# The output projection of the first 1024 tokens: moved wholly to the end of the recurrence

## The chip, the cores and the metric

The kernel runs on one core of a Trainium2 chip. The metric is the device time of one execution in microseconds (us), given as the median of several runs. The projections and the products of the MLP are done on pairs of float16 numbers: an operand is split into a high and a low part, and three products (high x high, low x high, high x low) stand for one product in float32.

## The reference

One layer of a hybrid encoder over 2048 tokens of width 1024:

```python
h = rmsnorm(x, norm_mix_g[l])
proj = h @ w_in[l]
u, dq, dk, dv, cq, cf, ci, cg = split_projection(proj)
y_a = s5_mixer(u, ...)          # 256 columns
y_b = diff_attention(...)       # 6 heads, 384 columns
y_c = hgrn2_mixer(cq, cf, ci, cg, ...)   # 6 heads, 384 columns, a recurrence over chunks of tokens
mix = jnp.concatenate([y_a, y_b, y_c], axis=-1)
x = x + (mix @ w_out[l])
h = rmsnorm(x, norm_ffn_g[l])
x = x + conv_glu_ffn(h, w_up[l], w_gate[l], conv_w[l], conv_b[l], w_down[l])
return rmsnorm(x, final_norm_g)
```

The change concerns `x + mix @ w_out` for tokens 0 to 1023, and the sums of squares that the second `rmsnorm` needs of them.

## The kernel before

**Two streams.** The program is written as two streams that a helper, `weave` (L2067), interleaves step by step by given weights. The left stream, `fore`, holds the input projections and attention, first for the queries of tokens 0 to 1023, then for those of 1024 to 2047. The right stream holds the S5 layer, the recurrence (`phase_hgrn`) and the tail (`phase_tail`: output projection, gated MLP, final norm). A step of the recurrence has weight 2.5, one of the tail 1.0, one unit of attention's second half 0.62, times `K.pace`, which is 1.8 in the head of the tail and 1.0 otherwise. A scheduler in the framework then fixes the order of instructions on every engine, the program order being the priority. DMAs are issued nearly all from SP's queue, in its order; among them are attention's transposing copies (L900).

**The recurrence** works in 12 units: three pairs of heads (`pr`), each with four chunks of 512 tokens (`j`), unit u = 4 pr + j. A unit has `proj`, `pre` and `fin`; `fin` stores its part of the mix at `Yd[5 + pr]` (L1360). After the loop `rest()` does `fin(10)`, `pre(11)` and `fin(11)`. Its pools: `g_w` (one weight buffer), `g_st` (one buffer for a raw weight), `g_h` (two buffers for the input), `g_3` and `g_2` (small tiles, tags `vn`, `x` and so on), and one PSUM buffer `g_pj` for projections.

**The mix** lies in DRAM as `Yd`: eight blocks of 128 columns, high and low part, by token. Blocks 0 and 1 are S5's, 2 to 4 attention's (one for each pair of heads), 5 to 7 the recurrence's. The weights `w_out` are used as q = 0 to 3 (two blocks each) and n = 0, 1 (512 output columns each); a pair (n, q) is one load of 512 KB and one split into high and low (`K.split`: a pass on ScalarE, L54, and one on VectorE, L62).

**`early_mix`** is woven with `rest()` and uses the recurrence's pools. It takes tokens 0 to 511 and q = 0, 1, 3 (`EARLY`). It loads two tiles of `Yd` (`o_ye`, 12 loads) into the `g_h` buffers, six weight pairs, and then goes over n and four token tiles: 18 matmuls into the one PSUM buffer (`o_pe`, L1409), an eviction that adds x (`o_re`, L1414), and a store into a side area of `Xd` (rows from 2048 on, L1417). `until(2)` before it waits, in program order, until two of attention's head pairs have been stored.

**The tail's head, `first`,** starts with the missing q = 2 for tokens 0 to 511 (`project(0, ...)`), onto the partial sums loaded back from `Xd` (`residual`, L1457). Then `project(1, ...)` does all four q for tokens 512 to 1023. `project` holds four PSUM banks at a time, loads `Yd` and `w_out` anew for every (n, q), and ends with `onto`: an eviction into `o_r` (L1500) and a sum of squares on ScalarE (`squares`, L1588). `keep` (L1941) stores the finished rows in `Xd`. `scaled` does the normalisation, `turned` transposes by TensorE (L1531), and the sinks `left` and `right` make of the first and second 512 tokens the seven operand quarters `f_q` of a Strassen-like product (`f_join`, L1554). `left` runs between the halves of `project(1)`. Then `activations` starts: 22 x 7 products of 12 matmuls each (`f_pm`, L98) and the elementwise work between them.

After `activations` comes the down product (`f_pd`, L1772) for these tokens, then the same for tokens 1024 to 2047, whose projection (`second`) also uses `project`.

**Room.** The tail's pools lie on the side of SBUF that the recurrence's pools held, with waits tile by tile; `f_q` comes first, where `g_w`, `g_st` and `g_h` were.

Of the kernel before, what the change touches and what calls it, by code (L numbers as in the profile page):

```python
# [18 lines left out]
S = 2048  # L19
# [14 lines left out]
EARLY = [0, 1, 3]  # L34
# [978 lines left out]
def phase_hgrn(K, Hd, w_in, lb_logits, norm_g, Yd, spare):  # L1013
# [9 lines left out]
    with ExitStack() as es:  # L1023
# [349 lines left out]
        yield from weave(rest(), 18, spare(pj, st, wp, hp, w3, w2), 6)  # L1373


def early_mix(K, x, w_out, Yd, Xd, pj, st, wp, hp, w3, w2):

    nc = K.nc
    y = []
    for a in range(2):  # L1380
        t = hp.tile([128, 2, KD, 256], F16, tag="h", name="o_ye")
        for k in [k for q in EARLY for k in (2 * q, 2 * q + 1)]:
            nc.sync.dma_start(out=t[:, :, k], in_=Yd[k, :, :, 256 * a:256 * a + 256])
        y.append(t)
    w4 = wp.tile([128, 4, 2, 2, 512], F16, tag="w", name="o_we")
    ws = [w4[:, i] for i in range(4)]
    ws += [w2.tile([128, 2, 2, 512], F16, tag="x", name="o_wx") for _ in range(2 * len(EARLY) - 4)]
    for i, w in enumerate(ws):
        n, q = divmod(i, len(EARLY))
        q = EARLY[q]  # L1390
# [6 lines left out]
    for n in range(2):  # L1397
        cc = slice(512 * n, 512 * n + 512)
        for t in range(4):
            rows = slice(128 * t, 128 * t + 128)  # L1400
            tk = slice(128 * (t % 2), 128 * (t % 2) + 128)
            r = w3.tile([128, 512], F32, tag="vn", name="o_re")
            nc.sync.dma_start(out=r, in_=x[0, rows, cc])
            ps = pj.tile([128, 512], F32, tag="j", name="o_pe")
            i = 0
            for q, w in zip(EARLY, ws[len(EARLY) * n:]):
                for k in range(2):
                    for a, b in ((0, 0), (0, 1), (1, 0)):
                        nc.tensor.matmul(  # L1409
                            out=ps, lhsT=y[t // 2][:, a, 2 * q + k, tk], rhs=w[:, b, k, :],  # L1410
                            start=(i == 0), stop=(i == 6 * len(EARLY) - 1),
                        )
                        i += 1
            nc.vector.scalar_tensor_tensor(  # L1414
                out=r, in0=ps, scalar=IWS / YS, in1=r, op0=ALU.mult, op1=ALU.add
            )
            nc.sync.dma_start(out=Xd[S + 128 * t:S + 128 * t + 128, cc], in_=r)  # L1417
            yield 1


def phase_tail(K, x, Xd, Yd, Ad, w_out, norm_g, W, conv_w, conv_b, w_down, final_g, out, es,
               ahead):

    tc, nc = K.tc, K.nc
# [690 lines left out]
```

## Time and profile before

| what | us |
|---|---|
| three timed runs | 2808.53, 2815.44, 2818.59 |
| their median | 2815.44 |
| the profiled execution | 2795.69 |
| its span, first to last instruction | 2794.0 |
| TensorE matmuls busy in it | 2442.0 (87%) |
| VectorE busy | 2004.2 (72%) |
| ScalarE busy | 1222.2 (44%) |
| GpSimd busy | 1309.4 (47%) |
| mean granted TensorE clock | 0.931 of full speed |

The profile is of one execution, so its stages are measured on its own 2795.69 us. PE is TensorE's matmul stream and PEld its weight loads, DVE is VectorE, ACT ScalarE, POOL GpSimd, SPq the queue from which SyncE issues DMAs. In a row for a group of instructions the operands stand as output<-input by tile name, then the shapes and a count. In a timeline the first number is the start, the second the length, and brackets hold the idle time before and what ended it. In a table by stage every engine has its busy time and, in parentheses, its instructions; behind them stand the granted clock, the mean busy share of the 16 DMA engines, and the GB/s that they moved. Matmuls are pipelined, so the length of one is longer than its distance from the next.

### The profile page before, as it was taken

The page shows a single profiled execution, that of the slowest core. Times are in us where ns is not written, and L with a number is a line of the kernel's source. Part 1 is how long each engine was busy: PE and PEld are TensorE (multiplying, and loading weights), DVE is VectorE, ACT ScalarE, POOL GpSimd, SP SyncE. Part 2 cuts the span into 40 slices and gives each one's busy share as a digit, 9 for nine tenths or more (in the row PEclk, how much of TensorE's full clock was granted, in tenths as well). Part 3 has the DMA queues.
Part 4 walks back from the last instruction along what each step waited for, and adds up shares of the span by engine and source line. Part 5 has one row for each costly group of instructions (what it writes and reads, how often), then busy time and mean ns, then how long its engine had stood idle before and what let it go on. Part 6 is the DMA issues. An engine that isn't in the chain of part 4 may idle for free. (4 is left out here: it accounts for less than half of the span.)

```text
span 2794.0 us, 42749 instructions
## 1 busy us (share of the span) xinstructions
PE 2442.0 (87%) x15438; PEld 1375.0 (49%) x15438; DVE 2004.2 (72%) x3893; ACT 1222.2 (44%) x2231; POOL 1309.4 (47%) x1095
## 2 busy tenths in 40 slices
PE   5998897989988888677998887859899999999998
PEld 3654546867766764243443333324344444444443
DVE  7466746789988897688779899975654855555575
ACT  5333344556645663565345555552234422222221
POOL 4788602334334432246666666631802344444180
PEclk8999998989989988788999999979999999999999
DMA  6675554555464656864455655587775655554733
GB/s 226 232 219 192 162 174 101 123 131 132 90 150 98 132 130 134 253 171 120 164 172 158 175 140 159 142 256 239 258 268 192 221 164 154 166 155 143 270 103 121
DMA packets 554533, 474.13 MB, mean 170 GB/s; under 512 B 276880, under 2 KB 432848, under 8 KB 553296
## 3 DMA queue, kind: packets, MB, share of 16 engines
q1 hardware_dynamic: 532144, 431.02, 54.1%
q10 hardware_dynamic: 22176, 40.38, 4.0%
q8 instruction: 121, 1.98, 0.3%
q14 instruction: 92, 0.75, 0.1%
HBM read 289.30 MB, written 127.93 MB: 149 GB/s over the span
## 5 line engine op out<-in xcount | busy, mean ns | idle before, releaser
L98 PE MATMUL f_pm<-f_q,f_w 128*128 128x512 f16 x3696 | 841.3, 387 | 37.9 <-DVE f_u L1837 21.7
L98 PEld LDWEIGHTS <-f_w 128*128 128x128 f16 x3696 | 363.7, 99 | 506.7 <-issue 90.4
L1772 PE MATMUL f_pd<-f_dw,f_da 128*128 128x512 f16 x1848 | 406.5, 383 | 11.7 <-DVE f_r L1750 10.4
L893 POOL TENSOR_TENSOR t_sc<-t_sc 128x1024 f16<-128x1024 f32 (+7 forms) x144 | 250.2, 1749 | 338.9 <-ACT t_sc L892 313.5
L1772 PEld LDWEIGHTS <-f_da 128*128 128x128 f16 x1848 | 181.8, 99 | 233.0 <-issue 18.5
L850 ACT ACTIVATE t_sc<-t_sc,t_nm 128x128 f32<-128x128 f32 (+7 forms) x192 | 229.1, 1195 | 99.1 <-DVE t_nm L845 91.7
L834 PE MATMUL t_ps<-t_k,t_q 96*128 96x512 f16 (+2 forms) x480 | 168.7, 377 | 99.0 <-DVE t_mx L838 86.6
L838 DVE CUSTOM_DVE_ANT_0 t_sc<-t_ps,t_base,t_mx 128x512 f32<-128x512 f32 (+3 forms) x288 | 185.1, 643 | 28.2 <-PE t_ps L834 21.5
L60 DVE TENSOR_TENSOR f_a<-f_t,f_a 128x512 f16<-128x512 f32 x132 | 148.1, 1129 | 46.1 <-ACT f_a L54 42.0
L98 PE MATMUL g_pq<-g_h,g_w 128*128 128x256 f16 x1152 | 158.6, 298 | 16.7 <-DVE g_sg L1162 10.6
L915 PE MATMUL t_po<-t_v,t_wt 128*128 128x64 f16 x2448 | 123.2, 201 | 56.4 <-DMA t_wt<-t_sc 48.7
L915 PEld LDWEIGHTS <-t_wt 128*128 128x128 f16 x2448 | 109.2, 104 | 123.1 <-DMA t_wt<-t_sc 67.0
L1837 POOL TENSOR_TENSOR f_t<-f_t,f_t 128x512 f32<-128x512 f32 x66 | 106.8, 1632 | 129.3 <-ACT f_a L54 108.3
L1487 PE MATMUL o_pm<-o_w,o_y 128*128 128x512 f16 x624 | 147.1, 394 | 19.9 <-DMA o_y<-Yd 14.1
L869 DVE SCALAR_TENSOR_TENSOR t_sc<-t_sc,t_a 128x1024 f32<-128x1024 f32 (+7 forms) x144 | 163.2, 1159 | 0.9
L1837 POOL TENSOR_TENSOR f_k<-f_k,f_k 128x512 f32<-128x512 f32 x88 | 124.7, 1417 | 73.2 <-ACT f_k L1869 68.3
L98 PE MATMUL g_pv<-g_w,g_h 128*128 128x256 f16 x1152 | 151.5, 288 | 8.0 <-ACT g_w L54 4.7
L62 DVE SCALAR_TENSOR_TENSOR f_dw<-f_db,f_dw 128x1536 f16<-128x1536 f32 (+1 forms) x36 | 104.1, 2910 | 73.8 <-ACT f_dw L54 73.7
L1837 POOL TENSOR_TENSOR f_db<-f_db 128x1536 f32<-128x1536 f32 (+1 forms) x32 | 128.2, 4044 | 60.6 <-DMA f_db<-in_w_down_dram 60.6
L892 ACT CAST t_sc<-t_sc 128x1024 f16<-128x1024 f32 (+7 forms) x144 | 112.1, 793 | 93.1 <-DVE t_sc L869 89.5
L54 ACT ACTIVATE f_w<-f_sum 128x512 f16<-128x512 f32 x110 | 69.2, 629 | 182.4 <-DVE f_sum L141 76.9
L54 ACT ACTIVATE f_a<-f_t 128x512 f16<-128x512 f32 x154 | 95.5, 628 | 114.5 <-POOL f_t L1837 56.6
(327 smaller groups left out, 4534.8 us busy)
## 6 DMA issues: line engine op xcount, KB each, us to landing
f_w<-Wd SPq DMA_DIRECT2D x231, 256.0 KB, 3.0
Wd<-f_w SPq DMA_DIRECT2D x154, 256.0 KB, 2.1
Ad<-f_a ACTq DMA_DIRECT2D x154, 256.0 KB, 2.8
f_da<-Ad SPq DMA_DIRECT2D x42, 768.0 KB, 4.4
g_h<-Hd SPq DMA_DIRECT2D x24, 1024.0 KB, 7.0
f_db<-in_w_down_dram SPq DMA_DIRECT2D x24, 768.0 KB, 10.5
o_wst<-in_w_out_dram SPq DMA_DIRECT2D x32, 512.0 KB, 5.4
o_y<-Yd SPq DMA_DIRECT2D x52, 256.0 KB, 4.7
```

The source lines that it names most:

```text
L54: nc.scalar.activation(out=hi, in_=src, func=AF.Copy, scale=scale)
L60: nc.vector.tensor_tensor(out=lo, in0=src, in1=hi, op=ALU.subtract)
L98: nc.tensor.matmul(out=out, lhsT=lhs(a, k), rhs=rhs(b, k), start=(n == 0), stop=(n == 3 * nk - 1))
L834: nc.tensor.matmul(out=ps[:, 0:k1 - k0], lhsT=qt[:, c, 128 * (i % 4):128 * (i % 4) + 128], rhs=H.k[:, c, k0:k1], start=True, stop=True,)
L838: V.tensor_tensor_reduce(out=sc[c][:, k0:k1], in0=ps[:, 0:k1 - k0], in1=bs[:, k0:k1], scale=1.0, scalar=-3e38 if j == 0 else mx[:, c, j - ...
L850: nc.scalar.activation(out=sc[c][:, 0:L], in_=sc[c][:, 0:L], func=AF.Exp, scale=SLOPES[h], bias=nm[:, c:c + 1], accum_out=H.la[:, c, n_:n_ ...
L869: V.scalar_tensor_tensor(out=sc[0][:, k0:k1], in0=sc[1][:, k0:k1], scalar=a[:, 1:2], in1=sc[0][:, k0:k1], op0=ALU.mult, op1=ALU.add,)
L893: nc.gpsimd.tensor_tensor(out=hl[:, LM + k0:LM + k1], in0=sc[0][:, k0:k1], in1=hl[:, k0:k1], op=ALU.subtract,)
L915: nc.tensor.matmul(out=po, lhsT=wt[:, w, b, :], rhs=vt[:, b, 64 * v:64 * v + 64], start=(b == 0 and w + v == 0), stop=(b == i and w == 1),)
L1487: nc.tensor.matmul(out=ps[t], lhsT=y[:, k, a, 128 * t:128 * t + 128], rhs=w[:, b, k, :], start=(q == qs[0] and i == 0), stop=(q == qs[-1] ...
L1772: nc.tensor.matmul(out=ps[t], lhsT=a[:, q, x, tk], rhs=w[:, y, q, :], start=(first and q + x + y == 0), stop=(last and q == n - 1 and y == 1),
L1837: eng.tensor_tensor(out=o, in0=a, in1=b, op=op)
```

## The change

`early_mix` now does the whole projection of tokens 0 to 1023: all four q, both chunks `c` of 512 tokens. The eight weight pairs are loaded and split once and stay on chip: four in the `g_w` buffer, two in a new pool `o_z`, two in the tag `x` of `g_2`. Each tile is 24 matmuls into the same single PSUM buffer, then the eviction that adds x, a sum of squares on ScalarE into a lasting tile `ss`, and a store of final rows in `Xd`. The `Yd` tiles of the second chunk take the two `g_h` buffers that the first chunk's had. It has 16 steps instead of 8, woven at 16 against the 18 of `rest()`, where it was 6. The tail's head has no projection left: it loads the eight row tiles back, takes the sums from `ss`, scales, turns and makes the quarters, `left` wholly before `right`. `until(3)` moves ahead of the early mix.

```diff
-        yield from weave(rest(), 18, spare(pj, st, wp, hp, w3, w2), 6)
+        more = pool("o_z", 1)
+        yield from weave(rest(), 18, spare(more, pj, st, wp, hp, w3, w2), 16)
...
     w4 = wp.tile([128, 4, 2, 2, 512], F16, tag="w", name="o_we")
     ws = [w4[:, i] for i in range(4)]
-    ws += [w2.tile([128, 2, 2, 512], F16, tag="x", name="o_wx") for _ in range(2 * len(EARLY) - 4)]
+    ws += [more.tile([128, 2, 2, 512], F16, tag=f"z{i}", name="o_wz") for i in range(2)]
+    ws += [w2.tile([128, 2, 2, 512], F16, tag="x", name="o_wx") for _ in range(2)]
     for i, w in enumerate(ws):
-        n, q = divmod(i, len(EARLY))
-        q = EARLY[q]
+        n, q = divmod(i, 4)
...
+    for c in range(2):
+        y = []
+        for a in range(2):
+            t = hp.tile([128, 2, KD, 256], F16, tag="h", name="o_ye")
+            t0 = CH * c + 256 * a
+            for k in range(KD):
+                nc.sync.dma_start(out=t[:, :, k], in_=Yd[k, :, :, t0:t0 + 256])
+            y.append(t)
+        for n in range(2):
+            cc = slice(512 * n, 512 * n + 512)
+            for t in range(4):
+                rows = slice(CH * c + 128 * t, CH * c + 128 * t + 128)
+                tk = slice(128 * (t % 2), 128 * (t % 2) + 128)
+                r = w3.tile([128, 512], F32, tag="vn", name="o_re")
+                nc.sync.dma_start(out=r, in_=x[0, rows, cc])
+                ps = pj.tile([128, 512], F32, tag="j", name="o_pe")
+                i = 0
+                for q in range(4):
+                    for k in range(2):
+                        for a, b in ((0, 0), (0, 1), (1, 0)):
+                            nc.tensor.matmul(
+                                out=ps, lhsT=y[t // 2][:, a, 2 * q + k, tk],
+                                rhs=ws[4 * n + q][:, b, k, :], start=(i == 0), stop=(i == 23),
+                            )
+                            i += 1
+                nc.vector.scalar_tensor_tensor(
+                    out=r, in0=ps, scalar=IWS / YS, in1=r, op0=ALU.mult, op1=ALU.add
+                )
+                sq = more.tile([128, 512], F16, tag="sq", name="o_sq")
+                nc.scalar.activation(
+                    out=sq, in_=r, func=AF.Square, scale=D ** -0.5, accum_out=ss[:, c, n, t:t + 1]
+                )
+                nc.sync.dma_start(out=Xd[rows, cc], in_=r)
+                yield 1
...
-                st, wp, yp = pool("f_st", 2), pool("f_w", 3), pool("o_y", 2)
-                tp, rp, fp = pool("f_t", 2), pool("f_r", 4), pool("f_f", 2)
+                rp, fp = pool("f_r", 8), pool("f_f", 2)
                 K.pace = 1.8
                 left, right = sinks(hc, fp, 4, 3)
-                r0, r1 = [], []
-                s0, s1 = sums(), sums()
-                yield from project(
-                    0, [q for q in range(4) if q not in EARLY], st, wp, yp, (pm,), onto(r0, s0, tp),
-                    lambda: r0.extend(residual(rp, Xd[S:S + CH])))
+                r0, r1 = [residual(rp, Xd[CH * c:CH * c + CH]) for c in range(2)]
                 xs = spread(hc, 1) + spread(hc, 3)
-                keep(r0, 0)
-                scaled(r0, xs, s0)
-                yield from project(1, range(4), st, wp, yp, (pm,), onto(r1, s1, tp),
-                                   lambda: r1.extend(residual(rp, x[0, CH:N])),
-                                   turned(xs, (pm,), left))
-                keep(r1, CH)
-                scaled(r1, r1, s1)
+                scaled(r0, xs, ss[:, 0])
+                scaled(r1, r1, ss[:, 1])
+                yield from turned(xs, (pm,), left)
                 yield sum(turned(r1, (pm,), right))
...
+    ss = const.tile([128, 2, 2, 4], F32, name="ss")
...
             def spare(*pools):
-                until(2)
-                yield from early_mix(K, x, w_out, Yd, Xd, *pools)
+                until(3)
+                yield from early_mix(K, x, w_out, Yd, Xd, ss, *pools)
...
-            until(3)
             yield None
```

More of the change, by code (lines that the diff above doesn't have):

```diff
@@ L33 @@
 SLOPES = [2.0 ** (-8.0 * (i + 1) / NH) for i in range(NH)]
-EARLY = [0, 1, 3]
 DOWN_PARTS = [3, 3, 3, 2]
@@ L1371, in rest, with early_mix @@
             yield from fin(11)
-        yield from weave(rest(), 18, spare(pj, st, wp, hp, w3, w2), 6)
-def early_mix(K, x, w_out, Yd, Xd, pj, st, wp, hp, w3, w2):
+        more = pool("o_z", 1)
+        yield from weave(rest(), 18, spare(more, pj, st, wp, hp, w3, w2), 16)
+def early_mix(K, x, w_out, Yd, Xd, ss, more, pj, st, wp, hp, w3, w2):
     nc = K.nc
[L1379 to L1384, printed above, removed]
     w4 = wp.tile([128, 4, 2, 2, 512], F16, tag="w", name="o_we")
     ws = [w4[:, i] for i in range(4)]
-    ws += [w2.tile([128, 2, 2, 512], F16, tag="x", name="o_wx") for _ in range(2 * len(EARLY) - 4)]
+    ws += [more.tile([128, 2, 2, 512], F16, tag=f"z{i}", name="o_wz") for i in range(2)]
+    ws += [w2.tile([128, 2, 2, 512], F16, tag="x", name="o_wx") for _ in range(2)]
     for i, w in enumerate(ws):
-        n, q = divmod(i, len(EARLY))
-        q = EARLY[q]
+        n, q = divmod(i, 4)
         f = st.tile([128, 2, 512], F32, tag="wst", name="o_wst")
@@ L1396, in early_mix @@
         K.split(w[:, 0], w[:, 1], f, WS)
[L1397 to L1418, printed above, removed]
@@ L1421, in phase_tail @@
-def phase_tail(K, x, Xd, Yd, Ad, w_out, norm_g, W, conv_w, conv_b, w_down, final_g, out, es,
+    for c in range(2):
[32 more added lines that the diff above has]
+                yield 1
@@ L1422, in phase_tail @@
+def phase_tail(K, x, Xd, ss, Yd, Ad, w_out, norm_g, W, conv_w, conv_b, w_down, final_g, out, es,
                ahead):
@@ L2014 @@
     Ud = tc.dram_tile([S, 256], F32, name="Ud")
-    Xd = tc.dram_tile([5 * CH, D], F32, name="Xd")
+    Xd = tc.dram_tile([S, D], F32, name="Xd")
+    ss = const.tile([128, 2, 2, 4], F32, name="ss")
     Ad = [[tc.dram_tile([128, MF // 2, 2, CH], F16, name=f"Ad{j}{i}") for i in range(7)]
@@ L2046, in spare @@
             def spare(*pools):
-                until(2)
-                yield from early_mix(K, x, w_out, Yd, Xd, *pools)
+                until(3)
+                yield from early_mix(K, x, w_out, Yd, Xd, ss, *pools)
             for _ in phase_hgrn(K, Hd, w_in, hgrn_lb_logits, hgrn_norm_g, Yd, spare):
                 yield LW[3]
-            until(3)
             yield None
-            for n in phase_tail(K, x, Xd, Yd, Ad, w_out, norm_ffn_g, W, conv_w, conv_b, w_down,
+            for n in phase_tail(K, x, Xd, ss, Yd, Ad, w_out, norm_ffn_g, W, conv_w, conv_b, w_down,
                                 final_norm_g, out, es, lambda: run(fore)):
```

## The prediction

> **What bounds the kernel now.** I read the page from the top (span, then the slices), then the busy times by stage, then single instructions of the stages that the change touches.
>
> ```profile
> span 2794.0 us, 42749 instructions
> ...
> PE   5998897989988888677998887859899999999998
> ```
>
> A slice is 70 us. TensorE leads almost everywhere; from slice 27 (about 1890 us) on it has nothing left to give. The dip in slices 15 to 18 is the place of this change: the recurrence's last units, then the tail's projection of tokens 0 to 1023, then the start of the tail's up products. I cut it into stages:
>
> ```profile
> core 0: us, PE busy (x) PEld busy (x) DVE busy (x) ACT busy (x) POOL busy (x), PEclk, DMA share, GB/s
> 1022.00:1057.00 35.00, 27.57 (x237) 16.49 (x237) 34.95 (x74) 21.67 (x36) 17.10 (x12) 0.76 0.67 163
> 1057.00:1102.00 45.00, 40.38 (x313) 22.85 (x313) 35.81 (x92) 16.48 (x27) 10.94 (x10) 0.96 0.56 141
> 1102.00:1140.00 38.00, 16.29 (x123) 7.59 (x124) 23.46 (x66) 13.52 (x23) 10.19 (x6) 0.60 0.61 115
> 1140.00:1190.00 50.00, 40.55 (x259) 18.79 (x259) 28.09 (x55) 27.41 (x47) 11.38 (x6) 0.86 1.03 306
> 1190.00:1236.00 46.00, 37.25 (x247) 19.88 (x246) 36.74 (x101) 28.47 (x58) 14.40 (x11) 0.93 0.62 174
> 1236.00:1287.00 51.00, 31.07 (x189) 17.65 (x189) 48.67 (x75) 31.45 (x58) 32.38 (x21) 0.70 0.46 112
> 1287.00:1450.00 163.00, 152.58 (x758) 69.04 (x758) 120.89 (x152) 68.60 (x117) 103.37 (x71) 0.99 0.49 160
> 1450.00:1815.00 365.00, 304.50 (x1753) 141.10 (x1752) 329.84 (x509) 197.72 (x330) 241.34 (x153) 0.94 0.56 158
> 1815.00:1861.00 46.00, 16.49 (x151) 8.65 (x150) 39.49 (x69) 25.11 (x35) 19.97 (x12) 0.62 0.80 238
> ```
>
> The reader is to see three limits. In 1022 to 1057 VectorE is full. In 1102 to 1140 nobody is: the last recurrence unit is a chain of dependent steps, TensorE idles 21.7 of 38 us. In 1140 to 1190 the DMA engines are full (share 1.03), with TensorE idle 9.5 us. From 1236 VectorE is full again (48.67 of 51), making the quarters `f_q`. From 1287 the up products run beside the second half of attention, and 1815 to 1861 is what is left of attention, with TensorE idle 29.5 us.
>
> **What is removed.** Both kernels issue 384 matmuls for these tokens: 144 + 48 + 192 before, 16 tiles of 24 after. Their price is that of one in a dense run:
>
> ```profile
> 1166.50 7.04 PE L1487 MATMUL o_pm<-o_w,o_y 128*128 128x512 f16 x24 [2.13 <-DMA o_y<-Yd]
> ...
> 1206.33 7.93 PE L1487 MATMUL o_pm<-o_w,o_y 128*128 128x512 f16 x36
> ...
> 1287.61 6.80 PE L98 MATMUL f_pm<-f_q,f_w 128*128 128x512 f16 x24
> ```
>
> 7.93/36 = 0.22 us (the listed 0.38 us of one is its latency). 240 matmuls, 240 x 0.22 = 53 us, leave the stages 1140 to 1236 and go to the end of the recurrence. Weight splits fall from 16 to 8, each 1.05 us of ScalarE (the next row) and 1.2 us of VectorE (a row further down), so 8.4 and 9.7 us go.
>
> ```profile
> L54 ACT ACTIVATE o_we<-o_wst x4: 1048/1054/1057, 1020.7 to 1049.3; 128x1024 f16<-128x1024 f32 x4
> ```
>
> The partial sums in `Xd` (written at L1417, read at L1457) stay one store and one load; the 8 stores of `keep` (L1941) go, since early_mix writes the final rows. Weight loads fall by 8 x 512 KB and `Yd` loads from 12 x 128 + 20 x 256 KB to 32 x 128 KB, which empties the DMA stage 1140 to 1190. The sums of squares, 16 on ScalarE, only move, from stages where it is busy 27.4 of 50 and 28.5 of 46 us to ones where it is busy 16.5 of 45 and 13.5 of 38; each hides under the next tile's matmuls, and the last one is on the path before and after alike. Their result now stays in the constant tile `ss`, so the normalisation of either chunk can start without waiting for a pass over loaded rows. `until(3)` costs nothing: the third attention pair, its last store below, was done 200 us earlier.
>
> ```profile
> 798.65 0.52 SPq L950 DMA_DIRECT2D Yd<-t_yo  x1
> ```
>
> **When the new early mix ends.** Its tiles today:
>
> ```profile
> 1052.90 1.21 DVE L62 SCALAR_TENSOR_TENSOR o_we<-o_wst,o_we 128x1024 f16<-128x1024 f32 x1
> 1056.67 0.68 DVE L1414 SCALAR_TENSOR_TENSOR o_re<-o_pe,o_re 128x512 f32<-128x512 f32 x1
> ...
> 1076.85 0.69 DVE L1414 SCALAR_TENSOR_TENSOR o_re<-o_pe,o_re 128x512 f32<-128x512 f32 x1 [0.43 <-PE o_pe L1409]
> 1087.93 0.68 DVE L1414 SCALAR_TENSOR_TENSOR o_re<-o_pe,o_re 128x512 f32<-128x512 f32 x1
> ...
> 1101.57 0.69 DVE L1414 SCALAR_TENSOR_TENSOR o_re<-o_pe,o_re 128x512 f32<-128x512 f32 x1 [0.95 <-PE o_pe L1409]
> ```
>
> Four weight tiles now gate the first output tile; the fourth is split at 1054.1, so tile 1 leaves PSUM at about 1057. From 1056.67 to 1101.57 six tiles of 18 matmuls took 7.5 us each; six more matmuls make 8.8 us. The recurrence ends at 1130, with its last store:
>
> ```profile
> 1129.95 0.53 SPq L1360 DMA_DIRECT2D Yd<-g_yo  x1
> ```
>
> Until then that gives 1 + 73/8.8 = 9.3 tiles. The other 6.7 run with attention alone: 24 x 0.22 = 5.3 us, 0.7 eviction, about 1 us of hand-over both ways (one PSUM buffer, `pj`), a tenth for attention: 7.6 us, 51 us in all. **End: 1181 us**, bounds 1153 (7.5 and 5.3 us a tile) and 1223 (the worst interval above, 11.1 us, for all 15). The second token chunk needs both `g_h` buffers back; its first eight loads go out while the last two tiles of the first chunk run, so they lie under TensorE work; uncovered, the eight would cost some 8 x 0.6 us of issue and a landing. On SP they stand in one queue with attention's transposes:
>
> ```profile
> L1383 SPq DMA_DIRECT2D o_ye<-Yd x12: 527/610/1162, 993.8 to 1024.1; - x12
> ```
>
> The early mix issued 12 + 6 + 8 + 8 = 34 DMAs there and issues 32 + 8 + 16 + 16 = 72; 38 more at up to 0.61 us are 23 us of SP's time over some 160 us. They hold up nothing as long as each is ready when its turn comes. A load that waits at SP's head for a buffer (`o_ye` for the first chunk's matmuls, `o_re` for a store) stops the transposes behind it, and with them attention's value matmuls; I price that with attention, below.
>
> **From there to dense up products.** Today the last projection matmuls end here
>
> ```profile
> 1225.82 0.59 PE L1487 MATMUL o_pm<-o_w,o_y 128*128 128x512 f16 x2
> ```
>
> at 1226.2 (the start of the last), and the products run densely from 1287.6: 61.4 us of norms, turns and quarters, VectorE-bound. None of it is removed. The chain gains a trip through DRAM:
>
> ```profile
> Xd<-o_re SPq DMA_DIRECT2D x8, 256.0 KB, 2.5
> o_r<-Xd SPq DMA_DIRECT2D x4, 512.0 KB, 6.9
> ```
>
> 2.5 + 6.9 = 9.4 us. `left`, which ran under the projection's second half, now runs behind it, but under that trip: 8 steps of 0.69 + 0.63 us on ScalarE are 10.6 us. I count 9.4 once (bounds 0, and 20 if the trip, `left` and later weight loads, whose room is now under `f_r`, add up). Dense products: 1181 + 61.4 + 9.4 = 1251.8, that is **36 us earlier**.
>
> ```profile
> L1562 ACT ACTIVATE f_q<-o_pt,o_g x16: 667/686/732, 1197.7 to 2134.6; 128x512 f32<-128x512 f32 x16
> ```
> and for the split behind each of them
> ```profile
> L54 ACT ACTIVATE f_q<-f_join x40: 612/630/675, 1201.6 to 2189.5; 128x512 f16<-128x512 f32 x40
> ```
>
> **What is given back.** Attention filled these stages. These rows count its score matmuls by stage (the second pair of columns is their weight loads):
>
> ```profile
> 1236.00:1287.00 51.00, 7.34 (x18) 1.94 (x19) 0.70 0.46 112
> 1287.00:1450.00 163.00, 4.07 (x11) 0.98 (x10) 0.99 0.49 160
> 1450.00:1815.00 365.00, 34.62 (x100) 9.60 (x99) 0.94 0.56 158
> 1815.00:1861.00 46.00, 8.52 (x16) 1.66 (x16) 0.62 0.80 238
> ```
>
> and these the up products `f_pm` in two of the stages:
>
> ```profile
> 1287.00:1450.00 163.00, 149.45 (x672) 22.50 (x33) 13.78 (x24) 0.99 0.49 160
> 1450.00:1815.00 365.00, 274.49 (x1120) 35.06 (x52) 23.50 (x41) 0.94 0.56 158
> ```
>
> In 36 us attention made 36 x 18/51 = 12.7 scores; they now fall beside the up products. With p for a product and s for a score, 163 = 672p + 11s and 365 = 1120p + 100s give s = 1.14 us. By the weave's sums 3.4 of the 12.7 stay until after the last up product: the new early mix adds 8 steps of 2.5, worth 20/0.62 = 32 units of attention, while the tail's head shrinks from 66 steps (10 projections of 5, and 16 for the two turns) to 16, at 1.8 x 0.62 worth 59 and 14; 13 units fewer, 3.8 units a score (212 units and 56 scores a head). In the rest stage a score takes 46/16 = 2.9 us. So 9.3 x 1.14 + 3.4 x 2.9 = 20.5 us come back (bounds 0, if they fit into idle time, and 12.7 x 2.9 = 37).
>
> **Sum:** 36 - 20.5 = 15.5 us. After 1861 nothing changes. The profiled execution took 2795.69 us (1.7 around its span), so 2780 on its scale; the median of the three timed runs is 2815.44, 19.75 higher, and I carry that over: **2800 us**.
>
> **Rivals.**
> *All or most of the gain stays* (18%). For it: 1287 to 1815 leaves VectorE idle 77 us and TensorE 71. Against: s = 1.14 is a measured slope. Gain 36, up to 55 if the early mix ends by 1160: 2760 to 2780.
> *Attention sets the end* (14%). The first down product waits until 1861 for attention's rest, not for the up products; if all 12.7 scores end there, 37 us come back and the time stays: 2816. For it: the idle TensorE in 1815 to 1861. Against: the weave ties both by program order.
> *A cold TensorE* (8%). After 1102 today the granted clock is 0.60, and the 24 matmuls at 1166 took 0.29 us each instead of 0.22. If the recurrence's end and one PSUM buffer keep it there, 6.7 x 24 x 0.07 = 11.3 us come on top of 1181; 4 us of gain are left, 2811. The clock of 0.96 in 1057 to 1102, with the same single buffer, speaks against it while the recurrence runs; no row shows the loop alone. The Trainium skill, page "TensorE: Matmul & The Clock Gate", section "A second HAM failure mode: psum-queue depth-cycling", says that short idle times between bursts of matmuls, one PSUM bank after another, make the clock fall and rise again. By that rule the loop after 1130 would suffer, and the change with it.
> *Slower: the early mix becomes the long pole* (18%). By my own count 6.7 of the 16 tiles run after the recurrence, not beside it, and the tail's first tiles lie on the room of `g_w`, `g_h` and the weights, so all of it waits for the last tile. VectorE is full in 1022 to 1057, and one tile waited 11.1 us for its eviction. A PSUM buffer that comes free late stops each next tile. At 11.1 us a tile the end is 1223, dense products start at 1294, 6 us later than now; with 3.4 scores at 2.9 us that is 16 us lost, 2831. It turns to a loss from about 1217, some 10.7 us a tile.
>
> **How the numbers follow.** The forecast, gains of 8 to 30 us, has 42%. A difference within 0.3%, 8.4 us, is about what a measurement of this kernel cannot tell from no change. Faster: 42 + 18 = 60%; same: 14 + 8 = 22%; slower: 18%. The range from 2765 to 2829 leaves out the best tenth and the worst.
>
> **What would show it.** Right: no `o_pm` before 1900, 16 evictions of `o_pe` ending near 1181, DMA share below 1 after 1140, the first dense `f_pm` near 1252, a rest of attention after the last up product of about 55 us. Wrong: evictions over 10 us apart, `f_pm` still starting near 1287, or a gain there that is gone by the first `f_pd`.

## The result and the profile after

| | before | after | ratio, 95% interval |
|---|---|---|---|
| first timing, median of 4 and 4 runs | 2811.99 us | 2786.99 us | 0.9922 [0.9898, 0.9946] |
| second timing, 24 and 6 runs | 2809.69 us | 2790.58 us | 0.9923 [0.9894, 0.9951] |

The change makes the kernel 19 to 25 us faster. 2800 had been forecast, in a range from 2765 to 2829. The profiled execution after took 2791.56 us. Span and TensorE's line by slices, on its page:

```profile
span 2789.9 us, 42696 instructions
...
PE   4998887989888889858888888869899999999998
```

The dip has become narrower: counted from 0, slices 15 to 18 read 8, 6, 7, 7 before and 9, 8, 5, 8 now; only slice 17, 1186 to 1256 us, is still low. The busy time of each engine by stages of the changed kernel (columns as in the tables by stage above: TensorE, its weight loads, VectorE, ScalarE, GpSimd, granted clock, DMA share, GB/s):

```profile
core 0: us, PE busy (x) PEld busy (x) DVE busy (x) ACT busy (x) POOL busy (x), PEclk, DMA share, GB/s
1029.00:1067.00 38.00, 32.39 (x260) 23.00 (x261) 37.24 (x76) 21.69 (x35) 20.04 (x15) 0.63 0.66 162
1067.00:1137.00 70.00, 62.64 (x461) 33.33 (x459) 45.05 (x116) 27.97 (x56) 8.52 (x6) 0.95 0.53 151
1137.00:1189.00 52.00, 45.82 (x267) 21.80 (x267) 26.20 (x72) 18.24 (x36) 11.26 (x7) 0.93 0.62 132
1189.00:1227.00 38.00, 20.00 (x176) 14.07 (x175) 27.38 (x66) 28.44 (x48) 20.42 (x14) 0.74 0.87 248
1227.00:1269.00 42.00, 20.39 (x117) 8.40 (x116) 41.38 (x72) 25.38 (x47) 25.13 (x16) 0.74 0.27 72
```

The stage in which the DMA engines were full (share 1.03) is gone, and TensorE is busy 62.6 of 70 us while the recurrence ends. What is left is the tail's head, 1189 to 1269: 80 us in which TensorE has 40 us of work, at the end with VectorE full (41.4 of 42).

**Stretches.** To compare the kernels I divide the time at four events which all of them have: the recurrence's ninth store (`g_yo`), the first up product of tokens 0 to 1023, the last of them, and the first matmul of the second projection. Stretch S1 lies between the first two of these, S2 is the up products, S3 the down product and its weights, S4 the rest. Tables by stage of before (its first profile), then of after; behind each, the same windows counting only attention's score matmuls (first pair of columns) and VectorE's work on their results (second pair):

```profile
960.37:1253.10 292.73, 227.64 (x1832) 137.82 (x1831) 227.33 (x539) 156.01 (x271) 105.23 (x74) 0.85 0.70 174
1253.10:1816.80 563.70, 478.82 (x2616) 219.55 (x2616) 486.36 (x719) 287.81 (x486) 365.25 (x237) 0.94 0.52 153
1816.80:2051.80 235.00, 194.10 (x991) 88.92 (x990) 143.66 (x169) 75.35 (x99) 99.81 (x37) 0.90 0.75 246
```
```profile
960.37:1253.10 292.73, 42.11 (x114) 75.47 (x114) 0.85 0.70 174
1253.10:1816.80 563.70, 44.30 (x124) 81.79 (x125) 0.94 0.52 153
1816.80:2051.80 235.00, 8.15 (x15) 12.23 (x18) 0.90 0.75 246
```
```profile
964.51:1226.60 262.09, 217.61 (x1729) 135.61 (x1728) 191.64 (x468) 135.94 (x239) 88.15 (x65) 0.86 0.63 158
1226.60:1814.60 588.00, 492.28 (x2717) 225.14 (x2717) 518.66 (x771) 301.79 (x512) 385.40 (x248) 0.93 0.51 150
1814.60:2049.90 235.30, 195.89 (x994) 89.44 (x993) 132.14 (x172) 72.80 (x96) 96.19 (x35) 0.91 0.76 248
```
```profile
964.51:1226.60 262.09, 32.22 (x100) 65.20 (x100) 0.86 0.63 158
1226.60:1814.60 588.00, 49.10 (x136) 89.62 (x136) 0.93 0.51 150
1814.60:2049.90 235.30, 8.60 (x17) 13.87 (x20) 0.91 0.76 248
```

S1 is 30.6 us shorter. S2 is 24.3 us longer, with 12 scores more in it (136 for 124). S3 is as long as before. In these profiles this trade is the change: S1 wins, S2 pays a good part back.

**How far the profiles carry.** In this pair S1 to S3 are 6.0 us shorter together. With one more profile of each (before 2813.13 us, after 2791.35) the means give S1 33.0 us shorter, S2 24.6 longer, S3 1.2 shorter, S4 0.5 shorter: 10 us. The timed gain is about twice that. The first profile of before, 2795.69 us, lies below every timed run of that kernel (2800.90 to 2824.16). The two profiles of before also differ, by 9.7 us, in the time ahead of S1, where TensorE runs the same matmuls in the same order nearly to its end: it took 960.37 and 970.09 us before, 964.51 and 960.27 after, and 954.9 to 970.1 over all profiles of this study. So stretches are compared below between profiles, and totals only between timed runs. Even so a profile is of one execution: those of runs 3 and 8 below took 8 and 12 us less than the median of their kernel, that of run 11 took 9 us more.

### The profile page after: what moved, and what is told of

The parts are those of the page before. It is cut to its first block, busy times and chain, and to the rows that moved or that the text cites. A ratio compares the mean times of both kernels' runs of the same rounds, so it can differ in the third digit from the quotient of the medians.

```text
span 2789.9 us, 42696 instructions
## 1 busy us (share of the span) xinstructions
PE 2447.5 (88%) x15438; PEld 1377.6 (49%) x15438; DVE 1988.5 (71%) x3877; ACT 1213.6 (44%) x2223; POOL 1308.1 (47%) x1095
## 5 line engine op out<-in xcount | busy, mean ns | idle before, releaser
L1779 PE MATMUL f_pd<-f_dw,f_da 128*128 128x512 f16 x1848 | 407.5, 383 | 17.4 <-DVE f_r L1757 12.7
L59 DVE TENSOR_TENSOR f_a<-f_t,f_a 128x512 f16<-128x512 f32 x132 | 138.8, 1058 | 44.9 <-ACT f_a L53 41.0
L868 DVE SCALAR_TENSOR_TENSOR t_sc<-t_sc,t_a 128x1024 f32<-128x1024 f32 (+7 forms) x144 | 166.4, 1181 | 1.0
L97 PEld LDWEIGHTS <-g_w 128*128 128x128 f16 x1152 | 121.4, 107 | 50.6 <-issue 21.0
```

The source lines that it names most:

```text
L59: nc.vector.tensor_tensor(out=lo, in0=src, in1=hi, op=ALU.subtract)
L97: nc.tensor.matmul(out=out, lhsT=lhs(a, k), rhs=rhs(b, k), start=(n == 0), stop=(n == 3 * nk - 1))
L868: V.scalar_tensor_tensor(out=sc[0][:, k0:k1], in0=sc[1][:, k0:k1], scalar=a[:, 1:2], in1=sc[0][:, k0:k1], op0=ALU.mult, op1=ALU.add,)
L1779: nc.tensor.matmul(out=ps[t], lhsT=a[:, q, x, tk], rhs=w[:, y, q, :], start=(first and q + x + y == 0), stop=(last and q == n - 1 and y == 1),
```

## The experiments

All are given with the theories' expectations. Ratios are to the kernel before, timed beside it. "The chunk variant" and "the two-buffer variant" are the second and the third.

**1. The kernel before, once more,** for a second profile.

> The kernel before, unchanged, profiled once more, because its first profile took 2795.69 us and its timed runs 2807 to 2819. Theory A (the end of attention's last unit releases the loads of f_db, and these set the end of the first half; the whole gain is how much earlier attention ends): this profile takes about 2810 us, its last store of t_yo comes some 10 to 20 us later than the 1947 us of the first profile, and the start of the second half's projection moves with it. Theory B (the early mix and the tail's head set the end, attention does not): the difference between the two profiles of before lies ahead of the first f_pm at 1253 or spread over all stages.

It took 2813.13 us. Of the 17.4 us that its span is longer, 13.0 lie ahead of the first up product (1266.1 us for 1253.1): Theory B. Its stretches are in the table at the end of this section.

**2. Only tokens 0 to 511 are finished early;** the tail projects tokens 512 to 1023 as before, beside attention.

```diff
-        yield from weave(rest(), 18, spare(more, pj, st, wp, hp, w3, w2), 16)
+        yield from weave(rest(), 18, spare(more, pj, st, wp, hp, w3, w2), 8)
...
-    for c in range(2):
+    for c in range(1):
...
-                r0, r1 = [residual(rp, Xd[CH * c:CH * c + CH]) for c in range(2)]
+                r0, r1 = residual(rp, Xd[0:CH]), []
+                s1 = sums()
                 xs = spread(hc, 1) + spread(hc, 3)
                 scaled(r0, xs, ss[:, 0])
-                scaled(r1, r1, ss[:, 1])
-                yield from turned(xs, (pm,), left)
+                yield from project(1, range(4), st, wp, yp, (pm,), onto(r1, s1, tp),
+                                   lambda: r1.extend(residual(rp, x[0, CH:N])),
+                                   turned(xs, (pm,), left))
+                keep(r1, CH)
+                scaled(r1, r1, s1)
```

> One part alone: only the first chunk of 512 tokens is wholly projected beside the recurrence (8 steps of 24 matmuls, sums kept on chip); the second chunk stays in the tail with its own loads and splits. Theory A (attention's end decides): the matmuls of 192 stay in the tail, attention fills the tail's head as before, gain of 0 to 8 us against before. Theory C (the saved splits and the emptied DMA stage are the gain): 2 of 8 saved splits and 4 of 20 saved loads of Yd stay saved, so a quarter of the 25 us, 6 us. Theory B (the start of the up products decides): project(1) with its 45 us must still run after the recurrence, gain below 10 us. A gain of 20 us or more would say that the second chunk's move is worth nothing.

2780.23 us, 0.9902 [0.9884, 0.9919]: at least the whole gain, with 48 of the 240 moved matmuls, and with 16 splits still. All three theories expected 10 us or less; the case of the last sentence came in. Its table by stage:

```profile
962.31:1228.60 266.29, 222.56 (x1758) 137.50 (x1757) 208.99 (x487) 150.35 (x261) 98.67 (x69) 0.84 0.69 175
1228.60:1801.30 572.70, 487.45 (x2689) 224.43 (x2688) 503.67 (x761) 291.61 (x496) 380.50 (x240) 0.93 0.51 152
```

The first product starts only 4 us later than with the whole change (S1 266 for 262), and S2 is 15 us shorter. The products run densely from 303.6 us behind the ninth store (304.9 with the whole change); attention has done 119 scores by then, for 112, and 10 of the 15 us are saved after it. The projection of tokens 512 to 1023 gives attention a place that the whole change takes away. So the second chunk's move, four fifths of the moved matmuls, was not shown to pay anything.

**3. The early tiles alternate between two PSUM buffers,** every second one from the recurrence's own pool `g_ps` (`pp`, handed to `early_mix`).

```diff
-                ps = pj.tile([128, 512], F32, tag="j", name="o_pe")
+                ps = (pp.tile([128, 512], F32, tag="g", name="o_pe") if t % 2
+                      else pj.tile([128, 512], F32, tag="j", name="o_pe"))
```

> The changed kernel with its 16 output tiles alternating between the one projection buffer and the recurrence's three PSUM buffers, so that a tile need not wait for the eviction before it. Theory B (the end of the early mix decides): tiles come 0.7 to 1.5 us closer, the early mix ends 8 to 15 us ahead of 1189.9 and the time falls by 8 to 15 us against the changed kernel, ratio to before 0.987. Theory A: the early mix ends earlier too, but attention's end does not move by more than 4 us, and the time is that of the changed kernel within 5 us, ratio 0.992.

2777.90 us, 0.989 [0.9872, 0.9908]. S1 falls to 242 us, S2 rises to 593: as Theory B has it, the early mix's end counts, though the interval still overlaps the changed kernel's. Run 9 repeats it and shows how.

**4. Attention is woven more densely into the up products.**

```diff
             K.pace = 1.0
+            K.pace = 0.85
             yield from activations(hc, 0, pooler(e1), pm, 1, 3, 5, 3, None)
```

> The changed kernel with attention's weight beside the up products lowered from 1.0 to 0.85, so attention gets 1/0.85 of the steps there and ends before the last up product instead of after it. Theory A: the last t_yo comes 15 to 40 us earlier, f_db loads start as much earlier up to what the staging of f_dst allows (it took 86 us from the last up product), and the time falls by 5 to 15 us against the changed kernel, ratio to before 0.987 to 0.990. Theory B: the up products are held back by attention, their end moves later by the work taken in, and the time is the same or up to 10 us more, ratio 0.992 to 0.996.

2809.40 us, 1.0007 [0.9994, 1.002]: the gain is gone. Timeline of SP's queue in this run, attention's last store and the first load of raw down weights, then its table by stage:

```profile
1857.53 0.52 SPq L949 DMA_DIRECT2D Yd<-t_yo  x1
...
1926.82 10.50 SPq L1733 DMA_DIRECT2D f_db<-in_w_down_dram  x8
```
```profile
1224.70:1836.80 612.10, 502.81 (x2908) 232.67 (x2908) 551.30 (x827) 325.50 (x542) 403.14 (x253) 0.92 0.51 150
1836.80:2066.90 230.10, 181.65 (x803) 80.86 (x802) 103.36 (x116) 53.50 (x68) 81.09 (x29) 0.88 0.68 240
```

In SP's queue of the changed kernel the load of `f_db` follows attention's last store at once, as if released by it:

```profile
1940.67 8.25 SPq L949 DMA_DIRECT2D Yd<-t_yo  x2
1948.97 9.06 SPq L1733 DMA_DIRECT2D f_db<-in_w_down_dram  x8
```

In run 4 attention's last store comes 91 us sooner (the second of the two above is at 1948.4), the load 22 us sooner (44 us sooner counted from the last up product, which comes at 1836.8 us for 1814.6), and S3 shrinks by 5 us. S2 grows by 24. Attention's end did not set the end of this half; Theory A falls as an account of the time. Theory B has the mechanism, but the loss is about twice the 10 us that it allowed.

**5 to 8** were timed together, to part what the moved matmuls bring from what the saved loads and splits bring. Run 5 is the changed kernel.

> The changed kernel itself, timed beside the next three on one chip. Theory I (idle account): up to the second half's projection the time is TensorE's work plus its idle time; finishing tokens 0 to 511 early fills idle time of the recurrence, and moving tokens 512 to 1023 only swaps one filler of TensorE (attention scores) for another. Then this kernel is within 8 us of the variant that moves tokens 0 to 511 alone (2780.2 us measured), 2780 to 2788 us. Theory J (loads and splits): the gain comes from the loads, splits and stores that no longer stand at the tail's start; the second 512 tokens save most of them, so this kernel should be faster than that variant by 8 us or more.

2790.58 us, 0.9923 [0.9894, 0.9951]. Neither theory's figure came: the whole change is 10 us slower than the chunk variant's 2780.23 (6 us by the ratios, with intervals that overlap), where Theory I allowed 8 and Theory J wanted it 8 us faster.

**6. Eight more weight tiles are loaded and split** beside the second chunk's tiles, for nothing.

```diff
+                if c == 1:
+                    again = more.tile([128, 2, 512], F16, tag="again", name="o_wa")
+                    f = st.tile([128, 2, 512], F32, tag="wst", name="o_wst")
+                    nc.sync.dma_start(out=f, in_=w_out[0, 256 * t:256 * t + 256, cc]...)
+                    K.split(again, again, f, WS)
```

> The changed kernel with eight more weight tiles of 512 KB loaded and split beside the tiles of tokens 512 to 1023; their result is not used. Theory J: the eight saved splits are worth 8.4 us of ScalarE and 9.7 us of VectorE, so the time rises by 8 to 15 us over the changed kernel. Theory I: the tiles of that stretch wait for one PSUM buffer and the splits lie beside them, so the time rises by 0 to 4 us.

2798.66 us, 0.9961 [0.9941, 0.9981], 8 us above the changed kernel, at the low end of Theory J's 8 to 15; the intervals overlap by a thousandth. The last early tile's matmuls end about 10 us later, and S1 is 10 us longer (272).

**7. The chunk variant with the loads, splits and stores of before put back** at the tail's start; their results are not used (the stores write the same rows again).

```diff
+                for n in range(2):
+                    y = yp.tile([128, 2, 2, CH], F16, tag="y", name="o_yj")
+                    for k in range(2):
+                        nc.sync.dma_start(out=y[:, k], in_=Yd[4 + k, :, :, 0:CH])
+                    f = st.tile([128, 2, 512], F32, tag="wst", name="o_wst")
+                    nc.sync.dma_start(out=f, in_=w_out[0, 512:768, 512 * n:512 * n + 512]...)
+                    w = wp.tile([128, 2, 2, 512], F16, tag="w", name="o_wj")
+                    K.split(w[:, 0], w[:, 1], f, WS)
+                keep(r0, 0)
                 scaled(r0, xs, ss[:, 0])
```

> The variant that moves tokens 0 to 511 alone, with what the kernel before had at the tail's start put back beside it except the 48 products: two weight tiles and their splits, 1 MB of Yd, and the 2 MB of stores of the finished rows (a second time, the same values). Theory J: it loses most of the 27 us, 2795 us or more. Theory I: the gain is the 48 products and the wait between them and the first transposes, so it stays within 6 us of that variant, 2780 to 2787 us.

2797.72 us, 0.9949 [0.993, 0.9968], 17 us above the chunk variant's medians. The first matmuls of the tail's projection, in TensorE's timeline of the chunk variant and then of this run, and the stage there, of the chunk variant and then of this run:

```profile
1141.33 13.18 PE L1494 MATMUL o_pm<-o_w,o_y 128*128 128x512 f16 x48 [8.08 <-ACT o_w L53]
```
```profile
1156.48 12.04 PE L1494 MATMUL o_pm<-o_w,o_y 128*128 128x512 f16 x48 [4.43 <-ACT o_w L53]
```
```profile
1123.00:1163.00 40.00, 29.02 (x158) 12.74 (x157) 26.16 (x62) 19.46 (x25) 14.27 (x7) 0.74 1.08 309
```
```profile
1120.00:1160.00 40.00, 17.17 (x85) 6.39 (x84) 28.25 (x70) 22.75 (x29) 17.36 (x9) 0.57 0.97 317
```

From the ninth store on that is 179.0 us and 197.4 us. The DMA engines are full in both (1.08 and 0.97), but here what is put back stands ahead of the projection's own weights: their first load is issued 19.7 us later, counted in the same way (at 1145.9 us, for 1129.4), and TensorE has 17 us of work in 40, for 29. More than half of the chunk variant's gain is this: no loads, splits and stores for tokens 0 to 511 at the tail's start. Theory J is right for the larger part and Theory I, with its limit of 6 us, wrong; the rest, about 12 us, is left for the 48 products and the wait around them, which were not moved alone.

**8. The chunk variant with two PSUM buffers.**

> Tokens 0 to 511 alone, with the early tiles alternating between two PSUM buffers. Theory I: the first tiles wait for weight splits and the recurrence, and the tail covers the rest with attention, so it is within 4 us of the variant with one buffer, 2776 to 2784 us. Rival (the single PSUM buffer paces the early tiles and its wait is on the path): 8 us or more faster than that variant, 2772 us or less.

2792.86 us, 0.9931 [0.9904, 0.9959]: no gain, and the interval meets the chunk variant's only at its edge. Theory I and the rival both miss: it is 12 us slower. The recurrence's last store comes 171.2 us after its ninth for 160.2, which fits the second buffer being borrowed from the recurrence, and the first up product follows at 278 us for 266. S2 is shorter (557), S3 longer (245). What the total makes of it is open; that the second buffer gains nothing here is clear.

**9 to 12** were timed together. **9. The two-buffer variant again.**

> The variant of the changed kernel whose early tiles alternate between two PSUM buffers, once more beside the next three. Theory K (what the runs so far leave): three terms. The span before the first up product falls by the moved work, the saved loads and splits (about 10 us) and here also by the wait for the one PSUM buffer; what attention has not done by then is paid back behind it, about 1 us a score. The first took 20 us off that span against the changed kernel, the second gave 6 us back, so this variant is 8 to 14 us faster than the changed kernel: 2776 to 2783 us, ratio 0.988 to 0.991. Rival (a mere scatter between calls): ratio 0.992 or above.

2779.68 us, 0.9889 [0.9869, 0.991], as in run 3 and as Theory K has it. The recurrence's last store in the changed kernel and here (SP's timelines), and here the stage of the last early tiles:

```profile
1135.45 0.56 SPq L1359 DMA_DIRECT2D Yd<-g_yo  x1
```
```profile
1149.87 0.57 SPq L1359 DMA_DIRECT2D Yd<-g_yo  x1
```
```profile
1128.00:1158.00 30.00, 29.55 (x250) 16.23 (x248) 18.28 (x59) 11.69 (x29) 4.89 (x4) 1.00 0.81 150
```

The recurrence ends 18 us later against its ninth store, yet the last early tile 29 us sooner (194.5 us behind that store for 223 to 224), with TensorE full where the changed kernel has it busy 45.8 of 52 us. S1 wins 19 us, S2 pays 6 back.

**10. The chunk variant again.**

> The variant that moves tokens 0 to 511 alone, beside the others on one chip. Theory K: it does not have the saved splits, but its second 512 tokens run beside attention scores in the tail; ratio 0.989 to 0.992, within 5 us of the two-buffer variant. Rival (the second 512 tokens pay once their buffer wait is gone): it is 8 us or more slower than the two-buffer variant.

2780.57 us, 0.9892 [0.9871, 0.9913]: within 1 us of the two-buffer variant, as Theory K has it. These two are the fastest kernels of the study. By the ratios they lie 6 to 9 us below the changed kernel, which was not timed in the same batch (run 12, its equal in time, was: 0.9925); the intervals still overlap. They reach it in different ways (S1 266 and S2 573, S1 243 and S2 595), and putting both together (run 8) did not add.

**11. The two-buffer variant with half of the `f_db` subtractions on VectorE.**

```diff
-                add(self.raw[b, c], self.raw[pair[0], c], self.raw[pair[1], c], ALU.subtract, P)
+                add(self.raw[b, c], self.raw[pair[0], c], self.raw[pair[1], c], ALU.subtract,
+                    P if c % 2 == 0 else V)
```

> The two-buffer variant, with half of the subtractions of down weights (odd cuts of f_db) on VectorE in place of GpSimd. Theory A (attention's end releases the f_db loads, and the 62 us of subtractions behind them set the start of the second projection): 10 us or more faster than the two-buffer variant. Theory K: TensorE has only 16 to 19 us of idle time in the 200 us of the down products, so the subtractions lie beside products; within 4 us of that variant.

2786.57 us, 0.9917 [0.9896, 0.9939]: 7 us slower where Theory A wanted 10 faster and Theory K allowed 4; the intervals overlap. S3 is 9 us longer (242.5 for 233.8). Between the first down product and the second projection TensorE waits longer for VectorE to evict down products (`f_r`); the waits of run 9 and then of this run, total us, times, longest:

```profile
PE f_pd L1780 <- DVE f_r L1758: 13.9, 3, 6.1
```
```profile
PE f_pd L1781 <- DVE f_r L1759: 23.0, 3, 12.8
```

The evictions stand in VectorE's order behind the subtractions, which run slowly there; the last section shows how slowly.

**12. The squares back in the tail.**

```diff
-                sq = more.tile([128, 512], F16, tag="sq", name="o_sq")
-                nc.scalar.activation(
-                    out=sq, in_=r, func=AF.Square, scale=D ** -0.5, accum_out=ss[:, c, n, t:t + 1]
-                )
...
+                for c, rs in enumerate((r0, r1)):
+                    for n in range(2):
+                        for t in range(4):
+                            squares(rs[t], n, ss[:, c, n, t:t + 1], tp, "t0")
                 scaled(r0, xs, ss[:, 0])
```

> The changed kernel with one part undone: the 16 squares with their sums are made by ScalarE in the tail, on the loaded rows, instead of behind each early tile. Theory K: 8 squares of 0.8 us now stand between the load of the rows and the first scale, 8 more before the second; 5 to 10 us slower than the changed kernel (2795 to 2800 us). Rival (they are hidden by the loads of other rows and by attention): within 3 us of the changed kernel, 2787 to 2793 us.

2790.07 us, 0.9925 [0.9906, 0.9944], the same as the changed kernel: the rival is right. The table by stage shows that this isn't because nothing moved:

```profile
958.73:1245.30 286.57, 225.18 (x1796) 140.06 (x1795) 210.58 (x512) 144.78 (x259) 98.22 (x71) 0.84 0.59 148
1245.30:1806.10 560.80, 480.87 (x2650) 220.08 (x2649) 487.04 (x724) 289.96 (x491) 368.83 (x239) 0.94 0.50 154
```

S1 grows by 25 us and S2 shrinks by 27: attention uses the longer S1 (111 scores in it for 100), and the up products get it back (126 beside them for 136). A late first product was no loss here, where attention filled the time.

**All of them** (us; the stretches by the profiles; idle is TensorE's in S1 to S3, their length less its busy time):

| kernel | S1 | S2 | S3 | idle | timed median |
|---|---|---|---|---|---|
| before, two profiles | 293, 296 | 564, 564 | 235, 240 | 191, 199 | 2807.6 to 2812.0 |
| after, two profiles | 262, 261 | 588, 588 | 235, 238 | 180, 180 | 2787.0, 2790.6 |
| 2, 10: first chunk alone | 266, 266 | 573, 573 | 235, 236 | 170, 168 | 2780.2, 2780.6 |
| 3, 9: two PSUM buffers | 242, 243 | 593, 595 | 236, 234 | 172, 170 | 2777.9, 2779.7 |
| 4: attention denser | 264 | 612 | 230 | 204 | 2809.4 |
| 6: eight more splits | 272 | 585 | 236 | 183 | 2798.7 |
| 7: 2 with the loads of before | 285 | 566 | 242 | 187 | 2797.7 |
| 8: 2 and 3 together | 278 | 557 | 245 | 186 | 2792.9 |
| 11: 3, subtractions shared | 245 | 593 | 243 | 184 | 2786.6 |
| 12: squares late | 287 | 561 | 239 | 183 | 2790.1 |

No single stretch orders the times; the idle time of TensorE over all three nearly does. That describes the runs and does not name a cause: TensorE's busy time is nearly the same in all (894 to 909 us), so its idle time follows the length. VectorE's busy time in S2 follows the length of S2 as well (472.7 of 557 us in run 8, 551.3 of 612 in run 4); which of the two engines makes a score cost time there was not tried.

## Why the prediction was right, and where it was off

The sign and its reason held: the projection's work leaves a stage full of DMAs for one with an idle TensorE, and attention takes part of that back. Step by step:

**What is removed.** No `o_pm` runs between the recurrence and the second projection, and the DMA share after 1137 us is 0.62, then 0.87 and 0.27. Eight loads and splits more beside the second chunk's tiles cost 8 us (run 6), with intervals that just overlap; what the saved ones cost in their old place is not shown by it. The squares could be had in either place for the same time (run 12).

**The end of the early mix.** Forecast 1181, found 1189.9 (the last eviction starts at 1189.2). The first tile left PSUM at 1067.7 and not at 1057: the split of the fourth weight ended at 1059.4, the tile's last matmuls, in turn with the recurrence's, at 1066.4, and VectorE had another split ahead of the eviction. The next ones came 6 to 11 us apart. After the recurrence they came 6.1 to 7.2 us apart, better than the 7.6 of the prediction, but for one at 14. Evictions, TensorE before the late one, and SP's queue:

```profile
1067.69 0.68 DVE L1417 SCALAR_TENSOR_TENSOR o_re<-o_pe,o_re 128x512 f32<-128x512 f32 x1
...
1169.00 0.69 DVE L1417 SCALAR_TENSOR_TENSOR o_re<-o_pe,o_re 128x512 f32<-128x512 f32 x1 [3.42 <-PE o_pe L1412]
...
1183.12 0.69 DVE L1417 SCALAR_TENSOR_TENSOR o_re<-o_pe,o_re 128x512 f32<-128x512 f32 x1 [8.69 <-PE o_pe L1412]
...
1189.24 0.69 DVE L1417 SCALAR_TENSOR_TENSOR o_re<-o_pe,o_re 128x512 f32<-128x512 f32 x1 [3.02 <-PE o_pe L1412]
```
```profile
1174.10 1.68 PE L914 MATMUL t_po<-t_v,t_wt 128*128 128x64 f16 x28 [4.49 <-DMA t_wt<-t_sc]
1175.59 4.90 PE L1412 MATMUL o_pe<-o_wz,o_ye 128*128 128x512 f16 x12
1180.32 2.75 PE L1412 MATMUL o_pe<-o_wx,o_ye 128*128 128x512 f16 x12
```
```profile
1159.88 5.67 SPq L1454 DMA_DIRECT2D f_cb<-in_conv_b_dram  x1
1165.67 2.37 SPq L1406 DMA_DIRECT2D o_re<-in_x_dram  x1
...
1168.62 2.29 SPq L899 DMA_TRANSPOSE t_wt<-t_sc  x1
```

The late tile's matmuls stand on TensorE behind attention's value matmuls, these wait 4.5 us for a transpose, and the transpose stands on SP behind a small load for the tail that took 5.7 us there. That is the chain that the prediction described for SP's queue, with another load at its head. After the wait twelve matmuls took 4.90 us and the next twelve 2.75.

Two readings of the prediction were off here, and its sum does not rest on them. The lower bound of 1153 is 1158 by its own numbers (5.3 tiles of 5.3 us after 1130). And the 11.1 us are the distance between two evictions, not a wait for one: that tile's matmuls ended at 1083.9, and its eviction came 4 us later.

**From there to dense products.** 61.4 + 9.4 us were forecast, 79.5 measured: the term that was counted at 9.4, with bounds 0 and 20, came out as 18.1. Dense products begin at 1269.4 and not at 1251.8, so 18 us earlier than before and not 36. Counted from the ninth store, in the mean of the two profiles of each kernel, it is 25 us. In both kernels four groups of 12 products come first, then a pause. The first group of before, then the first of after and its dense products:

```profile
1253.14 4.35 PE L98 MATMUL f_pm<-f_q,f_w 128*128 128x512 f16 x12 [1.11 <-ACT f_part L1572]
```
```profile
1226.56 5.00 PE L97 MATMUL f_pm<-f_q,f_w 128*128 128x512 f16 x12 [2.61 <-ACT f_part L1579]
...
1269.38 5.80 PE L97 MATMUL f_pm<-f_q,f_w 128*128 128x512 f16 x20 [7.17 <-ACT f_k L1871]
```

From the first group to the dense products it took 34.5 us before and 42.8 after, so of the 33 us that S1 wins 25 are left there. The reason lies behind the turns, which end at 1218.3 for 1246.9. From there to the dense products VectorE is full in both kernels, 40.6 of 40.7 us before and 50.5 of 51.1 after. Its work on the quarters is nearly the same (26 and 24 us); the rest, 27 us for 15, is attention's work and splits of up weights. So the step that was mis-sized is the way from the early mix's end to dense products: the prediction kept the old 61.4 us for a VectorE that takes in more of other work there.

**The give-back.** Of 12.7 scores, 9.3 were to fall beside the up products at 1.14 us and 3.4 behind them at 2.9 us, 20.5 us together. The scores between the first dense product and the last, before and then after:

```profile
1287.60:1816.80 529.20, 38.70 (x111) 73.11 (x111) 0.96 0.54 159
```
```profile
1269.40:1814.60 545.20, 43.84 (x124) 81.38 (x124) 0.94 0.53 156
```

13 scores more and 16.0 us more (16.4 in the second pair of profiles): 1.24 us a score, close to the fitted 1.14. The other 8.3 us that S2 is longer lie ahead of the dense products, above. The rest behind the last product was mis-sized: with 2 scores more it took 33 us to the first down product, not the 55 of the prediction's list, nor the 45 of before, and S3 is not longer at all. That "after 1861 nothing changes" is right only if counted from the last up product: the first down product comes 13.9 us earlier in the pair of profiles, and the second projection 1.9.

**The sum.** Counted from the ninth store, in the mean of the profiles, dense products come 25 us earlier, the last up product 8 and the end 10. Forecast were 36, 25 and 15.5. The head start was 11 us too large, the give-back beside the products 6 us too small (10.6 for 16), and the rest behind them, 9.9 us, cost nothing; these errors partly cancel. As the timed gain is about twice what the profiles show, it is in part luck that the forecast came near it.

**The scale.** 19.75 us were carried over from the profile to the median of three runs. The profile after lies within the timed runs of its kernel; that of before was an unusually quick one. On the medians of before that were measured beside the change, 2809.7 to 2812.0, the forecast gain of 15.5 us would have been 2794 to 2797. The remaining 4 to 10 us are the gain itself, which was larger than the sum; the profiles explain 10 of the 19 to 25 us, and what happened to the others is open.

**The rivals.** *All of the gain stays* did not come; S2 shows it. *Attention sets the end* is refuted by run 4. *A cold TensorE* is refuted for the place it named: after the recurrence the single-buffer loop ran at a granted clock of 0.93 in both profiles, with one slow group of twelve matmuls, above. *The early mix becomes the long pole* did not turn the sign, but its mechanism is real: without the wait for the one PSUM buffer S1 is 19 us shorter and the time 7 to 13 us less (2777.9 and 2779.7 for 2787.0 and 2790.6; 0.989 for 0.992 by the ratios, with intervals that overlap).

## What to carry to other kernels

Moving work into an idle stretch pays what the stretch's idle time takes up, less what the work that filled the old place now costs elsewhere; here the first fifth of the moved matmuls, with the loads that they spared, paid at least as much as all of it. Look at the total idle time of the bounding engine, not at the start of the next phase: a phase that started 25 us later cost nothing that the timing shows, where a filler used the time (run 12). And before believing that an event releases the next load, move it: here 91 us made a difference of 5.

## What the runs showed of the hardware

**VectorE beside GpSimd.** Splits of the same shape, in VectorE's timeline of the changed kernel: the first while GpSimd subtracts, the second when it has finished.

```profile
1980.64 3.46 DVE L61 SCALAR_TENSOR_TENSOR f_dw<-f_db,f_dw 128x1536 f16<-128x1536 f32 x1 [27.23 <-ACT f_dw L53]
...
2033.54 1.76 DVE L61 SCALAR_TENSOR_TENSOR f_dw<-f_db,f_dw 128x1536 f16<-128x1536 f32 x1 [4.79 <-ACT f_dw L53]
```

In run 11 the subtractions given to VectorE do the same, beside GpSimd's and alone:

```profile
1983.37 4.43 DVE L1846 TENSOR_TENSOR f_db<-f_db 128x1024 f32<-128x1024 f32 x1
...
1997.55 1.21 DVE L1846 TENSOR_TENSOR f_db<-f_db 128x1024 f32<-128x1024 f32 x1
```

Sharing two-operand work between these two engines gained no time there. The Trainium skill, page "SBUF — State Buffer", section "SBUF: two separate sides", says that of a VectorE instruction with two SBUF inputs and a GpSimd instruction that reads SBUF, the one that starts first holds the port pair they share for its whole length, and the other waits. The trace agrees: the 3.2 us between 4.43 and 1.21 fit a wait for one GpSimd subtraction, which took 3.4 to 4.9 us in that run.

**The granted clock with one PSUM buffer.** In the stage of the first early tiles the clock was 0.63 and 0.65 in the two profiles of the changed kernel and 0.83 in both of the two-buffer variant; later, 0.93 for the loop with one buffer and 1.00 with two. By the rule of the Trainium skill that the prediction weighed (page "TensorE: Matmul & The Clock Gate", section "A second HAM failure mode: psum-queue depth-cycling") the loop after the recurrence would be the cold one; here it was not. The low clock lay earlier, where TensorE is interrupted by waits for weight splits and by the recurrence as well as for the one PSUM buffer. It was higher there with the second buffer, so the one buffer may have a part in it; the parts were not tried one by one.
